# Five more pairs of merge gates by seven products ahead of the attention, and half of the sparse attention's scales on GpSimd

## The chip, the cores and the metric

The kernel runs on one core of a Trainium2 chip. The metric is the device time of one execution in microseconds (us), from the first to the last instruction and what lies around them. Before the change three runs gave 3183.8, 3187.17 and 3191.8 us; the median, 3187.17 us, is the time before. The engines are called PE (TensorE, matrix products), PEld (its weight loads), DVE (VectorE), ACT (ScalarE), POOL (GpSimd) and SP (SyncE, which here issues the transfers).

## The reference, cut to what matters

Two layers follow each other, each on 1024 tokens of width 1024. In a layer, four branches of width 512 (a gated MLP, a sparse attention in three parts, a forgetting attention, an attention on a memory) are projected up and merged under gates that come from the layer's normed input `h` alone:

```
h = rms_norm(x, g_pre)
parts = jnp.split(h @ w_in, IN_SPLITS, axis=-1)
...
ys = jnp.stack([y_a, y_b, y_c, y_m], axis=2)
up = jnp.einsum('bsnw,nwd->bsnd', ys, w_br)
gates = jax.nn.sigmoid(jnp.einsum('bsd,dne->bsne', h, w_gate))
merged = jnp.einsum('bsnd,bsnd->bsd', gates, up)
return x + rms_norm(merged @ w_o, g_post)
```

In the sparse attention the local part looks back over 256 keys, and its probabilities are weighed by a gate of their own:

```
o = g[..., 0:1] * o_cmp + g[..., 1:2] * o_sel + g[..., 2:3] * o_win
```

## The kernel before, in words

All products are in fp32 quality: a number is split in a high and a low part (`hi` by ACT, `lo = x - hi` by DVE or POOL), and three products stand for one (`mm3`, L244, L247, L248). A weight of 128 x 1024 is loaded by `weight` (512 KB), copied by ACT (L220) and subtracted on POOL (L222).

A layer has four stages. **Front** (`front`): norms and the memory's keys. **Gates** (`gates`, L1190 on): the values and projections that need only `h`, and merge gates made ahead of time. **Attention** (`attention`): the forgetting attention (`fox`), then the sparse attention (`nsa`) with the memory attention between. **Merge** (`merge`): the four branches are projected up (L244 to L248 into tiles `s`), multiplied by the gates' tanh and summed, then the output projection.

A merge gate is a 1024 x 128 column block of `w_gate` (branch n, block e, 32 of them) times all 1024 tokens. There are two ways to it. The plain way (`gate_early`, `proj`) takes 2 x 24 products of 128x512, 96 for a pair of neighbours. The other (`gate_pair`, L447) makes a pair by seven products of quarters instead of eight (Strassen's scheme as Winograd orders it): 7 x 12 = 84 products of 128x512, from sums of the tokens' quarters (made once a layer) and of the weights (`weight_sums`: four DVE sums, then seven ACT copies L438 and seven POOL subtractions L439 of 128x512 a pair). Both ways write the tanh to DRAM (`gate_store`), where the merge fetches it (L1281); a gate that no one made ahead is computed in the merge. `FRONT` lists the pairs made in the gates stage: nine of sixteen before. `FILL` lists what is computed beside the sparse attention, in this order: `u` (gated MLP, 96 products), `c`, `m`, `b` (output gates, 48 products each), and `w`, `y` (merge gates of branches 0 and 2, the plain way, 48 each). Before, that is 28 entries and 4 x 96 + 24 x 48 = 1536 products a layer; one gate (branch 2, block 5) is left to the merge.

A scheduler orders each engine's instructions when the program is built, earlier code first where it can. `follow` holds the fill back: each half projection of it (12 products) must stand behind a mark in the attention's score products, so that the fill is spread over the sparse attention's course and runs ahead of its even share by a few marks at most (`SLACK`).

A unit of the sparse attention (`nsa_unit`: one head, 256 queries) makes scores on PE (L565, L566, tiles `s`), masks and reduces them on DVE (L570, tiles `p`), takes exponentials on ACT (L575), multiplies by the reciprocal sum and the gate (`scale`, L640), turns blocks of `p` on PE (L597, tiles `pt`), splits them by ACT and DVE (L306, L308, tiles `pt2`) and multiplies them with the values (L609, tile `o`). There are 32 units a layer, and each scales the selected part and the local part (`win`), two query blocks each.

Of the kernel before, what the change touches and what calls it, by code (L numbers as in the profile page):

```python
# [187 lines left out]
STEP, SLACK = 4, 5.0  # L188


FILL = "u0 y6 y7 c0 y0 u1 w2 w3 m0 c1 b0 u2 w4 y1 m1 w5 c2 b1 u3 w6 w7 m2 y2 b2 c3 y3 m3 y4"

FRONT = [(0, 0)] + [(n, e) for n in (3, 1) for e in range(0, 8, 2)]


def ahead(items, n):
# [8 lines left out]
class Net:  # L207
# [412 lines left out]
        nc.gpsimd.tensor_add(t[r, 0], t[r, 0], t[r, 1])  # L620
        nc.sync.dma_start(dst[r, j * 256:(j + 1) * 256], t[r, 0])

    def scale(self, pcs, l, gate=(None, None)):

        nc = self.nc
        r = self.psm.tile([128, 2], F32, name="r")
        if len(pcs[0]) == len(pcs[1]) == 1:
            nc.vector.reciprocal(r, l[:, :, 0])
        elif len(pcs[0]) == 1:
            nc.vector.tensor_add(l[:, 1, 0:1], l[:, 1, 0:1], l[:, 1, 1:2])  # L630
            nc.vector.reciprocal(r, l[:, :, 0])
        else:
            nc.vector.tensor_add(r, l[:, :, 0], l[:, :, 1])
            nc.vector.reciprocal(r, r)
        for x in range(2):
            for t, b0, n in pcs[x]:
                if gate[x] is None:
                    nc.vector.tensor_scalar_mul(t[:, :n], t[:, :n], r[:, x:x + 1])  # L638
                else:
                    nc.vector.tensor_scalar(t[:, :n], t[:, :n], r[:, x:x + 1], gate[x], op0=OP.mult, op1=OP.mult)  # L640

    def put_values(self, name, h0):

# [309 lines left out]
    def nsa_unit(self, g, h, j, q, kd, kl, v, pc, dst):  # L953
        nc = self.nc
        l = self.psm.tile([128, 2, 2, 2], F32, name="l4")
        nm = self.psm.tile([128, 2, 2, 4], F32, name="nm4")
        sel, win = [], []
        for x in range(2):
            i = 2 * j + x
            def bias(b0, n, i=i):  # L960
                out = []
                m = min(n, i * 128 - b0)
                if m > 0:
                    s = self.selb[:, i - 4, b0 // 64:(b0 + m) // 64] if i >= 4 else self.zero16[:, :m // 64]
                    out.append((0, m, s[:, :, None].to_broadcast([128, m // 64, 64])))
                if b0 + n == (i + 1) * 128:
                    out.append((n - 128, 128, self.tri))
                return out
            sel.append(self.scores(q, kd[0], kl[0], i, 0, (i + 1) * 128, bias, nm[:, 0, x], l[:, 0, x]))
            k0 = max(0, i - 2) * 128  # L970
            wb = lambda b0, n, i=i: [(0, n, self.win[:, 384 - n:384])]
            win.append(self.scores(q, kd[1], kl[1], i, k0, (i + 1) * 128, wb, nm[:, 1, x], l[:, 1, x]))
        hd = (4 * g + h) * 3
        gate = lambda b: [self.sg[:, 2 * j + x, hd + 1 + b:hd + 2 + b] for x in range(2)]
        self.scale(sel, l[:, 0], gate(0))
        o = self.po.tile([128, 2, 256], F32, name="o")
        def blk(pcs, x, b):
            for t, b0, n in pcs[x]:
                if b0 <= b * 128 < b0 + n:
                    return t[:, b * 128 - b0:b * 128 - b0 + 128]  # L980
        it = lambda pcs, s, b, xs: dict(t=[(x, blk(pcs, x, b)) for x in xs], v=v[s][:, b, :])
        items = [dict(t=[(None, pc[:, 2 * j:2 * j + 2, :].rearrange("p i c -> p (i c)"))], v=self.vcm[:, :, g])]
        items += [it(sel, 0, b, (0, 1)) for b in range(2 * j + 1)] + [it(sel, 0, 2 * j + 1, (1,))]
        first = len(items)
        if j:
            items += [it(win, 1, 2 * j - 2, (0,)), it(win, 1, 2 * j - 1, (0, 1)),
                      it(win, 1, 2 * j + 1, (1,)), it(win, 1, 2 * j, (0, 1))]
        else:
            items += [it(win, 1, 1, (1,)), it(win, 1, 0, (0, 1))]
        items[first]["pre"] = lambda: self.scale(win, l[:, 1], gate(1))  # L990
        self.turn_and_sum(o, items)
        self.head_out(o, h % 2, j, dst)

# [205 lines left out]
    def gates(self):  # L1199
        sums = self.token_sums()  # L1200
        self.turn2 = 0
        next(sums)
        self.gmlp_w()
        self.gmlp_v(0)
        next(sums)
        self.gmlp_v(1)
        next(sums)
        self.put_values("cv0", 0)
        next(sums)
        self.put_values("cv1", 4)  # L1210
        next(sums, None)
        self.gmlp_sums()
        self.fox_proj(0)
        w = ahead((x for n, e in FRONT for x in self.weight_sums(f"g{n}{e}", f"g{n}{e + 1}")), 3)
        self.logits()
        for k, (n, e) in enumerate(FRONT):
            self.gate_pair(n, e, w, lambda: self.gmlp_mix(k - 1) if k else self.forget())

    def attention(self):
        self.cmp_proj()  # L1220
# [9 lines left out]
        for name in names:  # L1230
            h = int(name[1])
            if name[0] == "u":
                self.gmlp_u(h)
            elif name[0] in "wy":
                self.gate_early({"w": 0, "y": 2}[name[0]], h)
            else:
                self.gate_out(*{"c": (2, "cz"), "m": (3, "mz"), "b": (1, "bz")}[name[0]], h)
        self.pace = None
# [182 lines left out]
```

## Time and profile before

| what | us |
|---|---|
| median of three runs | 3187.17 |
| the profiled execution | 3185.2 |
| its span, first to last instruction | 3183.4 |
| PE busy in the span | 3071.0 |
| DVE, ACT, POOL busy | 1845.6, 1484.6, 1433.3 |

The busy time of PE is the time in which at least one product was under way. Products overlap, so a product's own duration (0.39 us for 128x512) is longer than its distance to the next one; what a product costs in a dense stretch is read from the starts of neighbours in the timeline. In the views by stretch a column gives an engine's busy time and its instructions; the two layers look alike, and stretches are given for the first: gates 195 to 390, forgetting attention about 449 to 720, sparse attention about 735 to 1310, merge to 1510.

### The profile page before, as it was taken

The numbers are of one execution on the slowest core, as the hardware profiler recorded it, in microseconds if no ns is written. First come the engines' busy times: TensorE is split into PE (matmuls) and PEld (weight loads), VectorE is DVE, ScalarE is ACT, GpSimd is POOL, SyncE is SP. The second block draws the span as 40 slices with busy tenths as digits, with TensorE's granted clock in tenths as the row PEclk, the third lists the DMA queues.
The fourth block names the chain that finished last, engine by engine and source line by source line (L and its number), as shares of the span: only waits on it lengthen the run. The fifth ranks groups of instructions, "written<-read, shape, count | busy, mean of one in ns | idle before, by whom it ended". The sixth has DMA issues, their size and how long they took to land.

```text
span 3183.4 us, 48317 instructions
## 1 busy us (share of the span) xinstructions
PE 3071.0 (96%) x16704; PEld 2633.9 (83%) x16704; DVE 1845.6 (58%) x4329; ACT 1484.6 (47%) x3393; POOL 1433.3 (45%) x1142
## 2 busy tenths in 40 slices
PE   6999999999999999999989999999999999999998
PEld 6978877887888888788989788888888888887888
DVE  6255447768666855336551554477685678554363
ACT  4333335556556555313443433455665556552132
POOL 6744445543232323258557444445432333232673
PEclk9999999999999999999999999999999999999999
DMA  6334485654334322456553344955632342225454
GB/s 206 101 116 133 135 249 172 189 179 131 103 104 147 109 90 93 149 173 197 193 180 105 113 135 146 276 160 175 192 123 83 107 153 99 98 90 184 156 185 140
DMA packets 251685, 466.96 MB, mean 147 GB/s; under 512 B 42512, under 2 KB 100880, under 8 KB 251440
## 3 DMA queue, kind: packets, MB, share of 16 engines
q1 hardware_dynamic: 251440, 463.87, 45.7%
q8 instruction: 132, 2.16, 0.3%
q14 instruction: 113, 0.93, 0.1%
HBM read 326.35 MB, written 137.43 MB: 146 GB/s over the span
## 4 chain that ended last, share of the span: by engine, by line
PE 78%; DVE 5%; POOL 5%; issue 4%; DMA 4%; ACT 3%; SPq 1%; DVEq 0%; POOLq 0%; ACTq 0%
PE pj L244 12%; PE pj L248 12%; PE pj L247 12%; PE s L247 6%; PE s L244 6%; PE s L248 6%; PE s L447 5%; PE o L609 5%; PE pt L597 5%; PE pj L447 4%; PE s L565 3%; PE s L566 3%; POOL wl L222 2%; DVE p L638 1%; POOL acc L1291 1%
## 5 line engine op out<-in xcount | busy, mean ns | idle before, releaser
L222 POOL TENSOR_TENSOR wl<-wr,wh 128x1024 fp32r<-128x1024 f32 (+1 forms) x216 | 515.9, 2392 | 646.5 <-ACT wh L220 562.5
L244 PE MATMUL pj<-hh,wh 128*128 128x512 f32 x1648 | 651.4, 395 | 2.6 <-DVE z L317 1.5
L248 PE MATMUL pj<-hh,wl 128*128 128x512 f32 x1648 | 651.4, 395 | 1.6 <-POOL wl L222 1.6
L247 PE MATMUL pj<-hl,wh 128*128 128x512 f32 x1648 | 649.7, 394 | 0.0
L575 ACT ACTIVATE p<-p,nm 128x384 f32<-128x384 f32 (+3 forms) x512 | 306.8, 601 | 204.3 <-DVE nm L570 201.3
L308 DVE TENSOR_TENSOR pt<-pt,pt 128x512 fp32r<-128x512 f32 (+1 forms) x464 | 292.4, 635 | 147.7 <-ACT pt L306 146.1
L248 PEld LDWEIGHTS pj<-hh,wl 128*128 128x128 f32 x1648 | 310.2, 188 | 61.6 <-POOL wl L222 2.5
L244 PEld LDWEIGHTS pj<-hh,wh 128*128 128x128 f32 x1648 | 310.8, 189 | 60.8 <-DVE z L317 2.4
L247 PEld LDWEIGHTS pj<-hl,wh 128*128 128x128 f32 x1648 | 310.4, 188 | 57.7
L306 ACT ACTIVATE pt<-pt 128x512 fp32r<-128x512 f32 (+1 forms) x464 | 251.9, 554 | 222.8 <-PE pt L597 162.2
L220 ACT ACTIVATE wh<-wr 128x1024 fp32r<-128x1024 f32 x216 | 228.4, 1057 | 248.0 <-PE pj L247 84.8
L609 PE MATMUL o<-pt,v 128*128 128x512 f32 (+1 forms) x864 | 245.2, 370 | 7.6 <-DVE pt L308 7.3
L618 POOL TENSOR_TENSOR yt<-yt 128x256 f32<-128x256 f32 x128 | 100.6, 786 | 292.7 <-ACT yt L617 232.8
L597 PE MATMUL pt<-ident,p 128*128 128x128 f32 x1488 | 230.9, 272 | 0.3
L597 PEld LDWEIGHTS pt<-ident,p 128*128 128x128 f32 x1488 | 184.9, 140 | 42.5 <-DVE pt L308 0.7
L244 PE MATMUL s<-yh,wh 128*128 128x512 f32 x512 | 199.9, 393 | 7.1 <-ACT yh L306 5.3
L247 PE MATMUL s<-yl,wh 128*128 128x512 f32 x512 | 201.0, 393 | 1.5 <-DVE yl L310 1.4
L248 PE MATMUL s<-yh,wl 128*128 128x512 f32 x512 | 200.3, 391 | 0.0
L565 PE MATMUL s<-kd,q 128*128 128x512 f32 (+2 forms) x512 | 187.5, 369 | 13.1 <-DVE nm L570 13.1
L566 PE MATMUL s<-kl,q 128*128 128x512 f32 (+2 forms) x512 | 175.7, 345 | 0.0
L609 PEld LDWEIGHTS o<-pt,v 128*128 128x128 f32 x864 | 147.6, 188 | 32.0 <-DVE pt L308 12.3
L640 DVE TENSOR_SCALAR p<-p,r,sg 128x384 f32<-128x384 f32 (+2 forms) x320 | 167.0, 577 | 1.7
(370 smaller groups left out, 7143.1 us busy)
## 6 DMA issues: line engine op xcount, KB each, us to landing
wr<-wt SPq DMA_DIRECT2D x234, 512.0 KB
th<-thd SPq DMA_DIRECT2D x124, 256.0 KB
thd<-gu SPq DMA_DIRECT2D x72, 256.0 KB
q<-rq SPq DMA_DIRECT2D x32, 512.0 KB
yf<-y SPq DMA_DIRECT2D x64, 256.0 KB
thd<-th SPq DMA_DIRECT2D x52, 256.0 KB
vd<-vs SPq DMA_DIRECT2D x48, 256.0 KB
v<-vd SPq DMA_DIRECT2D x24, 512.0 KB
```

Source lines behind the costliest of these rows:

```text
L222: nc.gpsimd.tensor_sub(lo[:, :n], raw[:, :n], hi.bitcast(F32)[:, :n])
L244: ins = nc.tensor.matmul(out, ah, bh, start=k == 0, stop=False)
L247: nc.tensor.matmul(out, ah, bl, start=False, stop=False)
L248: nc.tensor.matmul(out, al, bh, start=False, stop=k == n - 1)
L306: self.last_act = nc.scalar.activation(hi, src, AF.Copy, scale=scale)
L308: (nc.gpsimd if pool else nc.vector).tensor_sub(lo, src, hi.bitcast(F32))
L447: nc.tensor.matmul(out, w[a][:, k], t[b][:, k], start=start and k == x == 0, stop=k == 3 and x == 2, skip_group_check=True)
L565: self.mark(nc.tensor.matmul(ps[:, :w], q[:, tq], kd[:, b0:b0 + w], start=True, stop=False), 1 + n / 128)
L566: nc.tensor.matmul(ps[:, :w], q[:, tq], kl[:, b0:b0 + w], start=False, stop=True)
L575: nc.scalar.activation(p[:, :n], p[:, :n], AF.Exp, bias=init, scale=-1.0, accum_out=l[:, x:x + 1])
L597: nc.tensor.transpose(pt[:, off + x * 128:off + x * 128 + 128], src, self.ident)
L609: nc.tensor.matmul(o[:, :, t0:t0 + m], it["v"], w[:, :, off:off + m], start=first, stop=last)
```

## The change

`FRONT` gets five pairs more: fourteen of sixteen are made by seven products ahead of the attention. `FILL` loses the six `w` and three of the seven `y` entries; four `y` remain (blocks 6, 7, 4, 5 of branch 2), so all 32 gates are now made before the merge. The fill is 19 entries, 4 x 96 + 15 x 48 = 1104 products a layer. In `nsa_unit` the local part's two scales run on POOL (`pool=True`); its selected part stays on DVE.

```diff
-FILL = "u0 y6 y7 c0 y0 u1 w2 w3 m0 c1 b0 u2 w4 y1 m1 w5 c2 b1 u3 w6 w7 m2 y2 b2 c3 y3 m3 y4"
+FILL = "u0 y6 c0 u1 m0 c1 b0 u2 y7 m1 c2 b1 u3 m2 y4 b2 c3 m3 y5"
-FRONT = [(0, 0)] + [(n, e) for n in (3, 1) for e in range(0, 8, 2)]
+FRONT = [(n, e) for n in (0, 3, 1) for e in range(0, 8, 2)] + [(2, 0), (2, 2)]
...
-    def scale(self, pcs, l, gate=(None, None)):
+    def scale(self, pcs, l, gate=(None, None), pool=False):
         nc = self.nc
+        by = nc.gpsimd if pool else nc.vector
...
-                    nc.vector.tensor_scalar(t[:, :n], t[:, :n], r[:, x:x + 1], gate[x], op0=OP.mult, op1=OP.mult)
+                    by.tensor_scalar(t[:, :n], t[:, :n], r[:, x:x + 1], gate[x], op0=OP.mult, op1=OP.mult)
...
-        items[first]["pre"] = lambda: self.scale(win, l[:, 1], gate(1))
+        items[first]["pre"] = lambda: self.scale(win, l[:, 1], gate(1), pool=True)
...
-            self.gate_pair(n, e, w, lambda: self.gmlp_mix(k - 1) if k else self.forget())
+            self.gate_pair(n, e, w, lambda: self.gmlp_mix(k - 1) if 0 < k <= 8 else None if k else self.forget())
...
-            elif name[0] in "wy":
-                self.gate_early({"w": 0, "y": 2}[name[0]], h)
+            elif name[0] == "y":
+                self.gate_early(2, h)
```

The built order of PE in the middle of the sparse attention, before. Rows with `pj` are fill; `s` are scores, `pt` turned blocks, and `pt_8638` is the split copy of a turned bank.

```order
L565 MATMUL s<-kd,q 128x384
L566 MATMUL s<-kl,q 128x384
L244 MATMUL pj<-hh_501,wh 128x512
L247 MATMUL pj<-hl_503,wh 128x512
L248 MATMUL pj<-hh_501,wl 128x512
L597 MATMUL pt<-ident,p 128x128 x4
L565 MATMUL s<-kd,q 128x384
L566 MATMUL s<-kl,q 128x384
L244 MATMUL pj<-hh_501,wh 128x512
L247 MATMUL pj<-hl_503,wh 128x512
L605 MATMUL o<-pt_8638,vcm 128x2x128 x2
L609 MATMUL o<-pt_8638,v 128x512
```

The same engine in the middle of the sparse attention of the changed kernel, in one of the places where the fill has run out.

```order
L597 MATMUL pt<-ident,p 128x128 x8
L605 MATMUL o<-pt_9175,vcm 128x2x128 x2
L609 MATMUL o<-pt_9175,v 128x512
L565 MATMUL s<-kd,q 128x256
L566 MATMUL s<-kl,q 128x256
L565 MATMUL s<-kd,q 128x384
L566 MATMUL s<-kl,q 128x384
L609 MATMUL o<-pt_9186,v 128x512 x2
L597 MATMUL pt<-ident,p 128x128 x4
L609 MATMUL o<-pt_9196,v 128x512 x2
L597 MATMUL pt<-ident,p 128x128 x4
L565 MATMUL s<-kd,q 128x512
```

Where two or three fill products stood between a turned bank and the product that reads its split copy, only the unit's own scores and turns stand now.

The built order of POOL between the two groups of heads, before:

```order
L618 TENSOR_TENSOR yt<-yt 128x256
L620 TENSOR_TENSOR yt<-yt 64x256
L222 TENSOR_TENSOR wl<-wr,wh 128x1024
L618 TENSOR_TENSOR yt<-yt 128x256
L620 TENSOR_TENSOR yt<-yt 64x256
L618 TENSOR_TENSOR yt<-yt 128x256
L620 TENSOR_TENSOR yt<-yt 64x256
```

And there in the changed kernel:

```order
L618 TENSOR_TENSOR yt<-yt 128x256
L620 TENSOR_TENSOR yt<-yt 64x256
L641 TENSOR_SCALAR p<-p,r,sg 128x384 x2
L222 TENSOR_TENSOR wl<-wr,wh 128x1024
L618 TENSOR_TENSOR yt<-yt 128x256
L620 TENSOR_TENSOR yt<-yt 64x256
L918 TENSOR_TENSOR pc<-pc,cl 128x512
```

A unit's two local scales stand as a pair in POOL's queue, between the head outputs (`yt`) and the fill's weights (`wl`).

## Rows read from the trace of the kernel before

**Rows 1.** The page's first part: busy time, share and instructions of each engine.

```profile
PE 3071.0 (96%) x16704; PEld 2633.9 (83%) x16704; DVE 1845.6 (58%) x4329; ACT 1484.6 (47%) x3393; POOL 1433.3 (45%) x1142
```

**Rows 2.** Busy time by stretch; columns as its first line names them.

```profile
core 0: us, PE busy (x) PEld busy (x) DVE busy (x) ACT busy (x) POOL busy (x), PEclk, DMA share, GB/s
250.00:400.00 150.00, 150.00 (x705) 125.61 (x704) 70.65 (x130) 54.18 (x90) 71.02 (x57) 1.00 0.44 144
760.00:1300.00 540.00, 537.88 (x2817) 455.68 (x2818) 356.11 (x1011) 297.89 (x769) 161.02 (x126) 1.00 0.33 108
```

**Rows 3.** Timeline of PE in the gates: start us, us, engine, line, operation.

```profile
252.66 0.39 PE L447 MATMUL pj<-t3h,wh 128*128 128x512 f32 x1
252.89 0.39 PE L447 MATMUL pj<-t3l,wh 128*128 128x512 f32 x1
```

**Rows 4.** Groups by line, whole span: busy us, mean ns | idle before.

```profile
L439 POOL TENSOR_TENSOR wl<-ws,wh 128x512 fp32r<-128x512 f32 x72 | 98.1, 1375 | 103.6 <-ACT wh L438 67.3 <-PE s L447 33.0 <-PE pj L447 3.3
```

**Rows 5.** Groups by line and shape of DVE, 760 to 1300 us.

```profile
L308 DVE TENSOR_TENSOR pt<-pt,pt 128x512 fp32r<-128x512 f32 x94 | 64.3, 686 | 38.6 <-ACT pt L306 38.0
L640 DVE TENSOR_SCALAR p<-p,r,sg 128x384 f32<-128x384 f32 x64 | 38.1, 626 | 0.3
...
L570 DVE CUSTOM_DVE_ANT_1 p<-s,selb 128x512 f32<-128x512 f32 x32 | 22.0, 687 | 17.9 <-PE pt L597 12.7 <-PE s L566 4.4 <-PE pt L1152 0.5
...
L640 DVE TENSOR_SCALAR p<-p,r,sg 128x256 f32<-128x256 f32 x24 | 12.7, 530 | 0.0
...
L640 DVE TENSOR_SCALAR p<-p,r,sg 128x128 f32<-128x128 f32 x24 | 9.9, 412 | 0.3
...
L628 DVE RECIPROCAL r<-l 128x2 f32<-128x2 f32 x48 | 7.1, 157 | 2.5 <-ACT p L575 2.5
```

**Rows 6.** The scale's line, whole span: duration ns min/median/max.

```profile
L640 DVE TENSOR_SCALAR p<-p,r,sg x320: 331/478/2771, 764.2 to 2868.3; 128x384 f32<-128x384 f32 x64, 128x512 f32<-128x512 f32 x64, 128x128 f32<-128x128 f32 x32
```

**Rows 7.** Timeline of DVE at 775 us.

```profile
774.86 0.54 DVE L640 TENSOR_SCALAR p<-p,r,sg 128x512 f32<-128x512 f32 x1
...
775.65 3.38 DVE L640 TENSOR_SCALAR p<-p,r,sg 128x384 f32<-128x384 f32 x2
```

**Rows 8.** Timeline of POOL at 775 us.

```profile
775.25 2.75 POOL L222 TENSOR_TENSOR wl<-wr,wh 128x1024 fp32r<-128x1024 f32 x1 [12.53 <-PE pt L597]
```

**Rows 9.** Groups by line and shape of POOL, whole span.

```profile
L618 POOL TENSOR_TENSOR yt<-yt 128x256 f32<-128x256 f32 x128 | 100.6, 786 | 292.7 <-ACT yt L617 232.8 <-issue 58.3 <-POOL yt L620 1.5
...
L818 POOL MEMSET vcm<- 128x512 f32 x2 | 1.1, 526 | 0.0
```

**Rows 10.** Groups by line and shape of ACT, 760 to 1300 us.

```profile
L306 ACT ACTIVATE pt<-pt 128x512 fp32r<-128x512 f32 x92 | 54.1, 597 | 64.5 <-PE pt L597 47.1 <-PE o L609 6.4 <-PE pt L1152 6.1
L575 ACT ACTIVATE p<-p,nm 128x384 f32<-128x384 f32 x64 | 39.2, 613 | 19.2 <-DVE nm L570 18.9
L575 ACT ACTIVATE p<-p,nm 128x512 f32<-128x512 f32 x48 | 34.4, 718 | 19.5 <-DVE nm L570 19.5
...
L575 ACT ACTIVATION_READ_ACCUMULATOR p<-p,nm 128x1 f32 x160 | 30.3, 189 | 0.0
```

**Rows 11.** Timeline of PE at the end of the sparse attention.

```profile
1300.19 0.62 PE L609 MATMUL o<-pt,v 128*128 128x512 f32 x2
...
1304.83 0.74 PE L609 MATMUL o<-pt,v 128*128 128x512 f32 x2 [0.48 <-DVE pt L308]
...
1309.64 0.62 PE L609 MATMUL o<-pt,v 128*128 128x256 f32 x2 [0.56 <-DVE pt L308]
```

**Rows 12.** Timeline of PE at the start of the sparse attention.

```profile
721.31 0.51 PE L609 MATMUL o<-pt,v 128*128 128x256 f32 x2
...
727.31 0.45 PE L244 MATMUL pj<-hh,wh 128*128 128x512 f32 x1
```

**Rows 13.** Busy time by stretch where PE stands still and just behind.

```profile
1310.00:1313.00 3.00, 0.36 (x3) 0.10 (x1) 0.12 (x1) 1.79 (x4) 1.45 (x2) 1.00 0.00 0
1313.00:1316.50 3.50, 3.41 (x8) 2.38 (x9) 3.50 (x6) 3.49 (x7) 0.00 (x0) 0.52 0.48 150
```

## Prediction, made before the run

> **What bounds the kernel now.** First the page's busy shares [rows 1]: PE is busy in 96% of the span, no other engine in more than 58%. A share is an average over stages, so next the busy times by stretch [rows 2]. In the gates PE is busy in all of 150 us, with DVE, POOL and ACT at half or less. In the sparse attention it is busy in 537.9 of 540 us, DVE in 356.1, ACT in 297.9, POOL in 161.0. So both stages that the change touches are bound by PE today: work taken from PE there shortens the kernel, work moved between DVE and POOL does not by itself. Third, the timeline for the price of a product: a product of 128x512 is under way for 0.39 us, but its neighbour starts 0.227 us (252.89 less 252.66, with the rounding of the rows) behind it [rows 3]. A product that goes is worth 0.227, not 0.39.
>
> **The products.** Five pairs a layer change from 96 products to 84: 60 a layer and 120 in all, 120 x 0.227 = 27.2 us less. By place, for one layer: the gates gain 5 x 84 x 0.227 = 95.3 us, the fill loses 432 x 0.227 = 98.1 us, the merge loses the one gate left to it, 48 x 0.227 = 10.9 us. In the gates one pair lasts 84 x 0.227 = 19.1 us on PE; beside it POOL has seven subtractions of 1.375 us, 9.6 us [rows 4], and DVE and ACT have spare time at the shares of [rows 2], where nine such pairs already run back to back. I cost the new pairs' sums, copies and subtractions at nothing; without that cover the 9.6 us would still be half of what PE needs. Transfers: each pair loads the same two weights as before, earlier, through the same SP queue, and its four tanh tiles are stored either way; only the gate that the merge used to make adds two stores and two loads of 256 KB a layer. DMA is busy 0.44 of its time in the gates [rows 2], so I cost that at nothing too.
>
> **The scales.** 64 a layer go from DVE to POOL: 48 of 128x384, 8 of 128x256, 8 of 128x128, at 626, 530 and 412 ns [rows 5], 37.6 us less on DVE in each sparse attention. POOL's price for this operation is in no row. Below: writing 128x512 without reading took 526 ns; above: two inputs and 128x256 took 786 ns and 128x512 took 1375 [rows 4, 9], so 1.08 for 128x384. I take 0.9 us, near the subtractions, between 0.4 and 1.1. POOL's load is then 161 + 58 us less nine weights, still under half of its time. The scale stands between exponential and turn: by the built order, at the spacing of the rows, the turn of a local tile comes 28 us of PE work behind the score product (median of 128; 7.7 us at the least). The chain has a reduction, an exponential, a reciprocal and two scales, some 3.5 us. So the move costs PE nothing unless POOL's queue is late by several us; behind a scale in it stand head outputs and fill weights, which PE needs much later. At 0.4 or 1.1 us the sum is the same.
>
> The Trainium skill ("GPSIMD Engine Reference", section 4.1, Engine selection) says that GpSimd is about twice as slow as DVE with two inputs and roughly at line rate with one. By it the scale would take nearer the lower end, and the sum would be unchanged; no run so far shows it.
>
> **What the fill hid.** This is the term that decides. The fill falls from 1536 to 1104 products, and `follow` spreads it evenly over the score products; so where a unit has more to wait for than its share of fill covers, PE has nothing else. The built order shows it: in the first layer's sparse attention there are now nine places where 4 to 8 us of attention stand without a fill product, 54.0 us of issue together, by the spacings of the rows; before there was one of 4.9 us, and the last units at the end, which both kernels have. In such a place a bank is turned, copied by ACT in 0.60 us and subtracted by DVE in 0.69 [rows 5, 10], and the product that reads it stands 0.8 to 1.5 us of PE work behind the turn.
>
> Its price has three rows of evidence. (a) The end of the sparse attention today: from 1300.19 to the last `o` product at 1309.64, which ends its issue by 1309.98, 6.6 us of issue took 9.8 us, 0.48 lost for each us [rows 11]. There DVE has nothing else to do. (b) The one place in mid-stage: 4.9 us of issue took 6.0 (721.31 to 727.31), 0.22 [rows 12]. (c) The place of 8.2 us whose order the section on the change shows, walked by hand: behind the copy of its third bank ACT has two exponentials (0.61 + 0.19 + 0.72 + 0.19), then DVE two reciprocals (0.31), two scales (0.48 + 0.54), a reduction (0.69) and only then the fourth bank's subtraction (0.69), 4.4 us; PE has 2.0 us of its own work until the product that needs it. It is late by 2.4 us, and behind it DVE keeps up: 0.28 or 0.29 for each us. I take 0.28, from the very kind of place in question: 54.0 x 0.28 = 15.1 us a layer, 30.2 in two, less 2 x 1.1 that the one place of today loses: 28 us more waiting. Bounds: nothing, if banks and scores happen to be ready, and 0.48, which gives 51.8 - 2.2 = 50 us.
>
> **The sum** against the profiled execution, 3185.2 us: -27.2 + 28 = +1, so 3186. The median of the three runs lies 2.0 above that execution, so 3188 us: no change that can be told. For this kernel about 0.3% (9.6 us) is what a measurement can tell from none, 3177.6 to 3196.7.
>
> **Rivals.**
>
> *The fill was not needed.* The waits of PE in the sparse attention are 2 us of 540 today, DVE has a third of its time free [rows 2] and loses 38 us more of work. If the places without fill lose only what today's mid-stage place (b) loses or less (0 to 0.22, 0 to 22 us), the time is 3160 to 3182; with half of (b), 3185.2 - 27.2 + 10 + 2 = 3170. For it: the subtractions and scores mostly come well ahead of their readers. Against it: (a) and (c). Chance 0.30.
>
> *PE stands bare and slows down besides.* One mechanism, at the nine places of each layer: they cost (a)'s 0.48, 50 us, and the longer stops bring the lower clock. Today PE stands from 1310 to 1313 us, and the granted clock is 0.52 in the 3.5 us behind [rows 13], the lower of its two levels (1.2 of 2.4 GHz) for most of it, some 1.7 us lost. Eighteen places with a third of them so punished add 10 us. The time: 3185.2 - 27.2 + 50 + 2 = 3210, with the clock 3220. It decides from 0.36 lost for each us on, where the waits pass the 37 us that make the sum slower by over 0.3%. Chance 0.27.
>
> *POOL's scales hold up DVE.* At 775.25 a subtraction of 2.75 us starts on POOL, and DVE's two scales that start at 775.65 take 3.38 us together [rows 7, 8], where the median of one is 0.478 and the longest 2.771 [rows 6]: they stand until POOL has done. If each new scale on POOL holds DVE for its 0.9 us, DVE gets 58 us of standing a layer for the 38 us of work it gave. Only what falls in the 54 of some 450 us without fill reaches PE: 7 us a layer. 3188 + 14 = 3202. Against it: the DVE reductions and bank subtractions read one input from PSUM, and their rows hardly spread. Chance 0.05.
>
> The Trainium skill ("SBUF — State Buffer", section Who interferes with whom) has this as an exclusive lock: a DVE instruction in a two-port mode, `tensor_scalar` among them, and a GpSimd instruction block each other fully. The trace agrees for the 2.75 us subtraction at 775.25 and the scale behind it; by that rule the third rival's 14 us would be the most it costs here.
>
> **How the numbers follow.** The wash, 3178 to 3197, has 0.38 and the first rival 0.30, the second 0.27, the third 0.05. Faster by over 0.3%: the first rival and a little of the wash, 0.33. Within 0.3%: the rest of the wash, 0.36. Slower: the second and third and a little of it, 0.31. The likeliest case's time is 3188; its own range is 3178 to 3197. To hold the time 8 times in 10 the range reaches into the first two rivals, 3163 to 3214.
>
> **What would show it.** Products of L447 go from 1512 to 2352, those of L244, L247 and L248 fall by 960, and the gates last 95 us longer a layer with PE busy throughout; if PE waits for `wl` or `wh` of L438 and L439 there, the cover fails. The sparse attention should take about 450 us plus some 15 of waits, where the waits of `o` L609 for `pt` L308 and of `s` L565 for `nm` L570 grow from 2 us to over 10. If these stay at 2 us, the first rival holds; at 25 with more stretches of lowered clock, the second. POOL's L641 should last about 0.9 us for 128x384, and no transposition should wait for it; if `pt` L597 waits for POOL, the step on the scales is wrong. What would make the whole wrong is a merge or a forgetting attention that changes by more than the 11 us of its gate.

## The result, and the profile after

The changed kernel takes 3224.8 us (median of 4 runs, 3223.2 to 3233.7), beside 3187.2 us for the kernel before: 1.0116 of it, 95% interval 1.0097 to 1.0135. It is slower by some 37 us, where 3188 was forecast, and outside the range of 3163 to 3214. Four runs of 4344 us and more (two of the kernel before, one each of those with 8 and 7 pairs further down) were slow as a whole and are in none of the medians.

The first part of the page, changed kernel; it answers to [rows 1]:

```profile
PE 3070.7 (95%) x16584; PEld 2622.1 (81%) x16584; DVE 1863.6 (58%) x4291; ACT 1510.5 (47%) x3453; POOL 1570.2 (49%) x1320
```

PE makes 120 products fewer and is busy for the same 3071 us, in a span of 3221.6 in place of 3183.4 us: it stands 150.9 us in place of 112.4, and products that stand alone or run at a lower clock last longer (the mean of L609 went from 370 to 380 ns). The busy times by stretch tell where it stands. First the same stretch of the gates as in [rows 2], then the sparse attention of the first layer from its first to its last score product, changed kernel:

```profile
core 0: us, PE busy (x) PEld busy (x) DVE busy (x) ACT busy (x) POOL busy (x), PEclk, DMA share, GB/s
250.00:400.00 150.00, 150.00 (x705) 125.62 (x704) 73.45 (x135) 54.63 (x95) 72.11 (x60) 1.00 0.41 135
...
818.10:1307.60 489.50, 464.37 (x2461) 388.62 (x2459) 356.08 (x1002) 294.76 (x819) 195.31 (x189) 0.99 0.33 104
```

And the second of these in the kernel before:

```profile
725.40:1282.60 557.20, 553.03 (x2910) 468.69 (x2909) 378.59 (x1064) 315.83 (x848) 173.83 (x138) 1.00 0.34 110
```

The gates are as dense as before. In the sparse attention PE stands 25.1 us, where it stood 4.2; DVE's share rises from 0.68 to 0.73, though it has 22.5 us less to do, because the stage got shorter by 67.7 us.

What PE waits for most in that stretch, changed kernel (who waits <- for whom: us in all, times, the longest):

```profile
PE o L609 <- DVE pt L308: 10.8, 7, 3.7
PE s L565 <- DVE nm L570: 4.3, 5, 1.5
PE o L605 <- DVE pt L308: 4.3, 5, 1.6
PE s L901 <- DVE pc L903: 2.1, 1, 2.1
```

These four are 21.5 of the 25.1 us, and all of them are waits for DVE: the split of a turned bank (L308), the reduction that frees a bank of scores (L570), the masking of the compressed scores (L903). None is a wait for a scale on POOL.

To set stage against stage, the distance of each product to the next one is split into its issue (0.227 us for 128x512, less for the smaller ones, from the dense stretches) and the rest, at full and at lowered clock apart. The waits of this table are thus more than PE's standing: what a product takes beyond its issue counts too. This is worked out from all rows of PE in both traces; the first layer's merge reaches to the second layer's gates. Change from before to after, in us, first layer / second layer:

| stage | issue | waits at full clock | waits at lowered clock |
|---|---|---|---|
| gates | +95.3 / +95.3 | -0.1 / -0.3 | 0 / 0 |
| forgetting attention | -2.7 / -2.7 | +0.9 / +1.6 | +1.1 / 0 |
| sparse attention | -100.7 / -100.3 | +28.0 / +28.4 | +5.0 / +6.5 |
| merge | -5.5 / -5.9 | -4.2 / -1.4 | +1.7 / -0.4 |

So the products went as counted, and of the 201 us of issue that the two sparse attentions were spared a third came back as waits, 67.9 us, while the gates took their 190.6 in full.

The longest single stop, at 901.7 us, shows how it comes about. Timeline of all engines but the weight loads, changed kernel (start us, us, engine, line, operation, [idle before <- releaser]):

```profile
895.19 1.48 POOL L641 TENSOR_SCALAR p<-p,r,sg 128x384 f32<-128x384 f32 x2 [2.87 <-DVE r L629]
895.25 4.60 DVE L641 TENSOR_SCALAR p<-p,r,sg 128x512 f32<-128x512 f32 x4
...
896.51 1.09 ACT L306 ACTIVATE pt<-pt 128x512 fp32r<-128x512 f32 x2 [0.26 <-PE pt L597]
...
896.64 2.47 POOL L222 TENSOR_TENSOR wl<-wr,wh 128x1024 fp32r<-128x1024 f32 x1
...
897.72 0.28 PE L566 MATMUL s<-kl,q 128*128 128x256 f32 x1
...
899.77 0.67 DVE L317 SCALAR_TENSOR_TENSOR z<-z,pj 128x512 f32<-128x512 f32 x1
900.37 0.68 DVE L1134 TENSOR_REDUCE mm<-s 128x2 f32<-128x512 f32 x1
...
900.97 1.27 DVE L308 TENSOR_TENSOR pt<-pt,pt 128x512 fp32r<-128x512 f32 x2
...
901.70 1.22 PE L609 MATMUL o<-pt,v 128*128 128x512 f32 x2 [3.70 <-DVE pt L308]
```

The bank that PE needs is turned at 896.5 and copied by ACT. DVE has four scales in its queue that last 4.60 us, then a step of an output gate (L317) and a reduction of the memory attention (L1134), and only then the bank's subtraction. PE has its own work until 898.0 and no fill behind it. The four scales last longer than the 2.5 us that four of 623 ns took on the mean in the kernel before; POOL's two scales and its subtraction of 2.47 us run at the same time, so POOL has a part in this stop.

The same in the 4 us ahead of four of the stops: DVE is busy in 0.90 to all of them, where its mean over the stage is 0.73. Busy time by stretch, changed kernel:

```profile
897.70:901.70 4.00, 0.30 (x4) 0.10 (x2) 4.00 (x6) 0.00 (x0) 2.59 (x2) 0.83 0.78 253
847.20:851.20 4.00, 0.97 (x7) 0.63 (x5) 4.00 (x6) 1.64 (x4) 3.55 (x3) 1.00 0.24 62
869.80:873.80 4.00, 2.66 (x18) 2.13 (x17) 3.61 (x9) 1.47 (x3) 2.71 (x3) 1.00 0.16 59
825.60:829.60 4.00, 1.88 (x12) 1.30 (x10) 4.00 (x10) 1.40 (x3) 1.45 (x3) 1.00 0.40 147
```

The granted clock of 0.83 in the first of them says that the lower of the two levels (1.2 and 2.4 GHz) set in while PE stood.

The scales, by line and shape in the sparse attention of the changed kernel: POOL's, then DVE's, which answer to [rows 5].

```profile
L641 POOL TENSOR_SCALAR p<-p,r,sg 128x384 f32<-128x384 f32 x46 | 36.6, 804 | 80.2 <-DVE r L629 46.4 <-DVE r L635 19.0 <-PE pt L597 7.5
...
L641 DVE TENSOR_SCALAR p<-p,r,sg 128x512 f32<-128x512 f32 x45 | 37.0, 834 | 0.5
```

In the kernel before DVE's 128x512 took 623 ns in the same stretch:

```profile
L640 DVE TENSOR_SCALAR p<-p,r,sg 128x512 f32<-128x512 f32 x45 | 27.4, 623 | 0.3
```

### The profile page after: what moved, and what is told of

Same layout as the page of the kernel before. It is cut to its first block, busy times and chain, and to the rows that moved or that the text cites. A ratio compares the mean times of both kernels' runs of the same rounds, so it can differ in the third digit from the quotient of the medians.

```text
span 3221.6 us, 48552 instructions
## 1 busy us (share of the span) xinstructions
PE 3070.7 (95%) x16584; PEld 2622.1 (81%) x16584; DVE 1863.6 (58%) x4291; ACT 1510.5 (47%) x3453; POOL 1570.2 (49%) x1320
## 4 chain that ended last, share of the span: by engine, by line
PE 74%; DVE 10%; issue 4%; DMA 4%; POOL 4%; ACT 3%; SPq 1%; DVEq 0%; POOLq 0%; ACTq 0%
PE pj L244 9%; PE s L447 9%; PE pj L247 9%; PE pj L248 9%; PE pj L447 6%; PE s L244 6%; PE s L247 6%; PE s L248 6%; PE o L609 4%; PE pt L597 4%; PE s L565 2%; PE s L566 2%; DVE p L641 1%; DVE pt L308 1%; POOL wl L222 1%
## 5 line engine op out<-in xcount | busy, mean ns | idle before, releaser
L222 POOL TENSOR_TENSOR wl<-wr,wh 128x1024 fp32r<-128x1024 f32 (+1 forms) x196 | 468.9, 2397 | 332.8 <-ACT wh L220 313.6
L244 PE MATMUL pj<-hh,wh 128*128 128x512 f32 x1328 | 526.9, 397 | 0.9 <-DVE z L317 0.9
L248 PE MATMUL pj<-hh,wl 128*128 128x512 f32 x1328 | 524.3, 395 | 0.0
L247 PE MATMUL pj<-hl,wh 128*128 128x512 f32 x1328 | 523.8, 394 | 0.0
L308 DVE TENSOR_TENSOR pt<-pt,pt 128x512 fp32r<-128x512 f32 (+1 forms) x464 | 290.9, 634 | 108.7 <-ACT pt L306 107.0
L220 ACT ACTIVATE wh<-wr 128x1024 fp32r<-128x1024 f32 x196 | 206.9, 1056 | 202.3 <-PE s L247 82.5
L248 PEld LDWEIGHTS pj<-hh,wl 128*128 128x128 f32 x1328 | 250.5, 189 | 50.0
L244 PEld LDWEIGHTS pj<-hh,wh 128*128 128x128 f32 x1328 | 251.4, 189 | 47.0 <-DVE z L317 1.3
L247 PEld LDWEIGHTS pj<-hl,wh 128*128 128x128 f32 x1328 | 251.0, 189 | 46.0
L609 PE MATMUL o<-pt,v 128*128 128x512 f32 (+1 forms) x864 | 253.9, 380 | 29.2 <-DVE pt L308 29.0
L597 PE MATMUL pt<-ident,p 128*128 128x128 f32 x1488 | 235.1, 275 | 0.3 <-DVE pt L308 0.3
L597 PEld LDWEIGHTS pt<-ident,p 128*128 128x128 f32 x1488 | 187.6, 141 | 43.8 <-issue 1.5
L439 POOL TENSOR_TENSOR wl<-ws,wh 128x512 fp32r<-128x512 f32 x112 | 149.7, 1348 | 134.7 <-ACT wh L438 98.2
L565 PE MATMUL s<-kd,q 128*128 128x512 f32 (+2 forms) x512 | 192.3, 378 | 20.8 <-DVE nm L570 19.1
L609 PEld LDWEIGHTS o<-pt,v 128*128 128x128 f32 x864 | 145.7, 191 | 54.7 <-DVE pt L308 30.4
L641 POOL TENSOR_SCALAR p<-p,r,sg 128x384 f32<-128x384 f32 (+2 forms) x128 | 95.3, 753 | 192.9 <-DVE r L629 117.2
```

Of the source, the lines that this page charges most:

```text
L220: nc.scalar.activation(hi, raw, AF.Copy)
L222: nc.gpsimd.tensor_sub(lo[:, :n], raw[:, :n], hi.bitcast(F32)[:, :n])
L244: ins = nc.tensor.matmul(out, ah, bh, start=k == 0, stop=False)
L247: nc.tensor.matmul(out, ah, bl, start=False, stop=False)
L248: nc.tensor.matmul(out, al, bh, start=False, stop=k == n - 1)
L308: (nc.gpsimd if pool else nc.vector).tensor_sub(lo, src, hi.bitcast(F32))
```

## The experiments

The theories: **A**, DVE's local backlog, which the fill covered, makes the waits. **B**, POOL's scales hold up DVE. **C**, the even spacing of the fill and not its amount. **E** (later), PE's order is too tight for the chain's latency, whatever DVE has to do. Each time is a median with its ratio to the kernel before on the same chip. DVE's load and the waits at full clock (above those of the kernel before) are of the sparse attention; the load is that of the first layer, the waits are of first / second, and a dash stands where they were not worked out.

| run | pairs | time | ratio, 95% interval | DVE us | waits us |
|---|---|---|---|---|---|
| before | 9 | 3187 | 1 | 378.6 | 0 |
| after | 14 | 3224.8 | 1.0116 (1.0097 to 1.0135) | 356.1 | 28.0 / 28.4 |
| scales back on DVE | 14 | 3233.3 | 1.0147 (1.0132 to 1.0162) | 376.9 | 33.7 / 31.4 |
| scales on POOL alone | 9 | 3191.9 | 1.0016 (1.0006 to 1.0026) | 352.5 | 1.6 / 1.1 |
| all scales on POOL | 14 | 3208.4 | 1.0069 (1.0049 to 1.0090) | 316.6 | 21.6 / 20.4 |
| SLACK 60 | 14 | 3221.7 | 1.0115 (1.0095 to 1.0136) | 351.5 | 26.8 / 27.9 |
| 10 pairs | 10 | 3196.0 | 1.0027 (1.0015 to 1.0038) | 375.2 | 6.5 / 5.4 |
| 11 pairs | 11 | 3204.3 | 1.0053 (1.0037 to 1.0069) | 371.1 | 12.4 / 12.8 |
| 12 pairs | 12 | 3217.0 | 1.0090 (1.0072 to 1.0107) | 371.1 | 20.4 / 17.4 |
| all scales on POOL | 11 | 3198.4 | 1.0034 (1.0022 to 1.0045) | 310.3 | 10.1 / 10.4 |
| no scales | 14 | 3201.5 | 1.0047 (1.0030 to 1.0064) | 306.8 | 19.5 / 19.1 |
| no scales | 9 | 3185.1 | 0.9989 (0.9976 to 1.0003) | 308.4 | -1.7 / -1.0 |
| no ranking | 14 | 3201.5 | 1.0042 (1.0026 to 1.0058) | 333.1 | 19.1 / 21.1 |
| neither | 14 | 3190.5 | 1.0013 (1.0003 to 1.0022) | 288.3 | 14.6 / 11.6 |
| scales made twice | 9 | 3200.6 | 1.0042 (1.0027 to 1.0057) | 421.6 | 8.8 / 9.5 |
| 8 pairs | 8 | 3183.4 | 0.9983 (0.9969 to 0.9997) | 375.5 | -2.8 / -3.1 |
| 7 pairs | 7 | 3171.8 | 0.9957 (0.9943 to 0.9970) | 379.7 | -1.1 / -1.0 |
| 6 pairs | 6 | 3182.6 | 0.9983 (0.9970 to 0.9996) | 365.4 | - |
| 5 pairs | 5 | 3199.5 | 1.0035 (1.0023 to 1.0047) | 375.3 | - |

### Each part alone

The changed kernel with the local scales back on DVE:

```diff
-        items[first]["pre"] = lambda: self.scale(win, l[:, 1], gate(1), pool=True)
+        items[first]["pre"] = lambda: self.scale(win, l[:, 1], gate(1))
```

> The changed kernel (14 pairs ahead) with one part undone: the local branch's 64 scales a layer are on DVE again. Theory A (too little fill is left beside the sparse attention, and what comes last there is DVE's chain): DVE gets back the 22 us a layer that it lost (378.6 us before, 356.6 after, in a sparse attention that is 67 us shorter), all of it in the same bare stretches, so it is no faster than the changed kernel: 3225 to 3250 us. Theory B (POOL's scales hold up DVE, whose own scales of 128x512 went from 617 to 834 ns): the waits of 33 us a layer go back to a few us, 3190 to 3200. PE's waits in a sparse attention: A 28 us or more at full clock, B under 15.

The kernel before with that line the other way round:

> The kernel before (9 pairs ahead) with the other part alone: the local branch's scales on POOL. Theory A: there is fill enough, 2 us of waits a layer cannot shrink by much, 3180 to 3190 us, no change that can be told. Theory B: the same 128 scales hold up DVE here too; part of it is covered by fill, still 3196 to 3210. DVE's scales of 128x512 should go from about 617 to about 830 ns by either.

And the changed kernel with the selected part's scales on POOL too:

```diff
-        self.scale(sel, l[:, 0], gate(0))
+        self.scale(sel, l[:, 0], gate(0), pool=True)
```

> The changed kernel with the selected branch's 96 scales a layer on POOL as well. DVE then has no scale left that POOL can hold up, and loses some 70 us of work a layer (48 at 834 ns, the rest at 0.5 to 0.7 us); POOL gets some 80 us more, 276 of 490 us. Theory A (fill): the bare stretches stay as they are, but DVE's chain in them is shorter by one or two scales of 0.8 us; a third to a half of the 33 us a layer comes back, 3190 to 3210 us. Theory B: nearly all comes back, 3162 to 3180. Third: POOL's queue (1.0 us for a scale of 128x512, head outputs ahead of it) is late, turns wait for POOL, 3225 to 3260.

Measured: 3233.3, 3191.9 and 3208.4 us. The first has 8 us more than the changed kernel, where B asked for some 30 less, so B falls as the cause; with 14 pairs the move to POOL did no harm. With 9 pairs it is 5 us slower. Both differences are within the 0.3% that the prediction takes for no change. DVE's scales of 128x512 went to 697 ns there, not to the 830 that both theories named. With all scales on POOL, 25 us come back of the 46 that the first run lost on the kernel before: A's half, not B's all. The third way in that expectation, POOL's queue late, did not come: no turn in the first layer's sparse attention waits for it.

### Places, not amount

```diff
-STEP, SLACK = 4, 5.0
+STEP, SLACK = 4, 60.0
```

> The changed kernel with the number SLACK that sets how early a fill product may stand ahead of its share raised from 5 to 60: the amount of fill is the same, its places differ. Theory C (not the amount but the even pacing makes the waits): by 15 us or more different from the changed kernel, 3190 to 3210. Theory A (the amount): as many bare stretches in other places, 3215 to 3245. Work is the same in both: same products, same scales.

Measured: 3221.7 us, the same as the changed kernel's. In the built order the first layer's bare stretches of 4 us and more are other ones: five from 11.7 to 16.5 us, 70.9 us of issue that lost 30.0 us, in place of nine up to 8.2 us, 54.0 us that lost 22.5. The loss for each microsecond is the same, 0.42. C falls, as far as this one other spacing can tell: it is the amount.

### Pairs one by one

From the kernel before, with all scales on DVE, one to three pairs of branch 0 go from the fill to the front (three shown):

```diff
-FILL = "u0 y6 y7 c0 y0 u1 w2 w3 m0 c1 b0 u2 w4 y1 m1 w5 c2 b1 u3 w6 w7 m2 y2 b2 c3 y3 m3 y4"
+FILL = "u0 y6 y7 c0 y0 u1 m0 c1 b0 u2 y1 m1 c2 b1 u3 m2 y2 b2 c3 y3 m3 y4"
-FRONT = [(0, 0)] + [(n, e) for n in (3, 1) for e in range(0, 8, 2)]
+FRONT = [(0, 0)] + [(n, e) for n in (3, 1) for e in range(0, 8, 2)] + [(0, 2), (0, 4), (0, 6)]
...
```

> The kernel before with one pair more ahead (10, the pair of gates 2 and 3 of branch 0), all scales on DVE. 24 products less, -5.4 us by count. Theory A1 (a place without fill costs from about 4 us on): in one layer's sparse attention the order has 14.1 us in such places, none before; at 0.42 lost per us, as the changed kernel's nine places showed (22.5 of 54.0), 11.8 us in two layers: +6, 3193. Theory A2 (each pair costs the same from the first on): (3233 - 3187) / 5 = 9.3 us for each: 3196. Theory D (fill is spare at first, the pair is worth its count): 3181.

> The kernel before with two pairs more ahead (11: gates 2, 3 and 6, 7 of branch 0), all scales on DVE; -10.9 us by count. A1: 4.1 us in places of 4 us and more, 3.4 us lost in two layers: -7, 3179. A2: +18.6, 3205. D: 3176. The runs with 10 and 11 pairs tell A1 from D, and the one with 11 tells A1 from A2.

> The kernel before with three pairs more ahead (12: gates 2 to 7 of branch 0), all scales on DVE; -16.3 us by count. A1: 20.8 us in places of 4 us and more, 17.5 lost in two layers: +1, 3188. A2: +28, 3215. D: 3170, if the shortage begins only behind this.

Measured: 3196.0, 3204.3, 3217.0 us; A2 (3196, 3205, 3215) on all three. A1 held for 10 pairs only by chance: with 11 pairs the order has a single bare stretch of 4 us, and the waits are 12.6 us a layer all the same. Divided by the pairs moved, the mean waits of the two layers at full clock are 6.0, 6.3 and 6.3 us a pair, and 6.5 with 14 pairs and the scales on DVE. That is the shape of the thing between 9 and 14 pairs: no threshold, but a price for each microsecond of fill from the first one on. A pair takes 19 to 23 us of issue out of each sparse attention, and some 0.3 of it comes back as waits.

With 11 pairs and all scales on POOL:

> 11 pairs ahead as in the run above, and all 160 scales a layer on POOL, as in the run of the changed kernel with all scales there, which took 25 us from the same 14 pairs with the scales on DVE. If DVE's load is what turns a bare stretch into a wait, the gain scales with the waits that are left: by A1 there is little to gain, 3175 to 3185; by A2 about 11 pairs' waits of some 29 us shrink by half, 3185 to 3195. If POOL's queue itself costs time where there is fill enough (the scales on POOL made the kernel with 9 pairs 5 us slower), up to 3200.

3198.4 us: 6 us less than with the scales on DVE, slower than before all the same. The waits at full clock shrink by a fifth, from 12.6 to 10.2 us a layer, and not by the half that A2 had here.

### DVE's load

Two kernels leave out the scaling (14 pairs and 9), one the ranking of blocks, one both:

```diff
-                else:
-                    by.tensor_scalar(t[:, :n], t[:, :n], r[:, x:x + 1], gate[x], op0=OP.mult, op1=OP.mult)
```

```diff
-        for i in range(4):
-            own = im[:, i, :, None].to_broadcast([128, 16, 16])
...
-            nc.vector.reduce_sum(rank[:, i, :], ge, axis=AX.X)
+        nc.vector.tensor_copy(rank, im)
```

> 14 pairs ahead, all scales on DVE as in the run that took 3233 us, and then the 160 scales a layer left out (the probabilities stay unnormalised): DVE loses some 92 us of work a layer, and nothing goes to POOL in its place. Each pair has so far cost 9.3 us from the tenth on, in waits of PE at products whose bank or score DVE had not come to; DVE was busy 0.87 of the 4 us ahead of these waits and 0.76 on the mean. Theory A (DVE's local backlog is what fill covered): of some 34 us of waits a layer two thirds go, 3180 to 3192 us. Rival E (the order is too tight for the chain's latency whatever DVE's load): less than a third goes, 3212 or more. If it comes out at the 3208 of the run with all scales on POOL, POOL's lock and latency cost nothing; below it, they do.

> The kernel before with its 160 scales a layer left out. A and E: waits were 2 us of 540, nothing to gain: 3180 to 3190. Together with the run above it gives the price of a pair where DVE is light: by A about (3186 - 3185) / 5, near 0 for each; by E it stays near 9.

> The changed kernel with the ranking of the blocks left out (20 operations at the start of each group of heads, 22 us of DVE a layer in two bursts; a copy stands in its place, so other blocks are selected). If only the bursts at the group starts cause the waits: 12 us a layer less, 3200. If the backlog is spread over all units: 4 us a layer or less, 3215 to 3222.

> 14 pairs ahead with the 160 scales a layer and the ranking both left out (unnormalised probabilities, other blocks selected): some 114 us of DVE work a layer less than with the scales on DVE. Theory A (DVE's backlog, bursts above all): no scales gave 32 us and no ranking 23 us where each was alone; if they add up, 3233 - 32 - 23 = 3178, with 3160 where all waits go. Rival E (what is left is the chain's latency, whatever DVE's load): the ranking adds little beside the scales, 3195 or more.

Measured: 3201.5, 3185.1, 3201.5 and 3190.5 us. Without scales, 32 of the 47 us that 14 pairs cost with the scales on DVE come back, and a pair costs (3201.5 - 3185.1) / 5 = 3.3 in place of 9.3 us. That is more than E allowed and less than A asked. It is also 7 us below the run with all scales on POOL, so by the expectation POOL's part costs something there, though 7 us is little to go by. The ranking, 23 us of DVE a layer in two bursts, gives 23 us, which is the number named for bursts alone; but the scales, spread over all units, gave 32 as well, so it is neither alone. With both gone 43 us come back, where the sum of the two was 55 and E's bound 38. A holds for the most part; some 13 us of waits a layer remain. What the stretch waits for then (both left out, 818 to 1300 us):

```profile
PE o L605 <- DVE pt L308: 5.3, 3, 3.7
PE s L899 <- DVE pc L901: 2.0, 1, 2.0
PE o L609 <- DVE pt L308: 1.6, 4, 0.5
PE s L565 <- DVE nm L570: 1.6, 4, 0.8
```

The waits on DVE of L609 and L565 are 3.2 us, where the changed kernel had 15.1; those for the first bank of a unit (L605) are no shorter. The longest of these has another cause than DVE's load (timeline of the same run):

```profile
1074.48 1.09 DVE L900 TENSOR_TENSOR pc<-s,cmask 128x256 f32<-128x256 f32 x3 [3.06 <-DMA cmask<-cmask]
1075.49 0.55 DVE L308 TENSOR_TENSOR pt<-pt,pt 128x384 fp32r<-128x384 f32 x1
...
1076.18 0.77 PE L605 MATMUL o<-pt,vcm 128*128 128x256 f32 x2 [3.65 <-DVE pt L308]
```

DVE itself stands for 3.06 us until the mask of the second group of heads (`cmask`) has come, and the bank's split stands behind that masking in its queue; it is busy in 1.72 of the 4 us ahead of the stop. The second layer has the same at 2656.7, with 1.60 us. The other remaining waits stay open: ahead of some DVE is full, ahead of others not.

The counter-test: the kernel before, its fill whole, with each scale made by two operations.

```diff
...
+                elif twice:
+                    nc.vector.tensor_scalar_mul(t[:, :n], t[:, :n], r[:, x:x + 1])
+                    nc.vector.tensor_scalar_mul(t[:, :n], t[:, :n], gate[x])
...
```

> The kernel before (9 pairs, all of its fill) with each of the 160 scales a layer made by two operations in place of one, on DVE: about 92 us of DVE work a layer more, 470 of 557 us. Theory A: DVE's share (0.84) is above that of the kernel with 14 pairs (0.76), so PE waits though the fill is whole; at the price that the scales had with 14 pairs (32 us for 2 x 92) at least 16 us a layer, 3219 or more. Theory F (fill hides DVE's chain as long as there is enough of it, whatever DVE's load): 3187 to 3195.

3200.6 us: above F's 3195 and well below A's 3219. The two operations are each shorter than the one, so DVE got 43 us more a layer, not 92; A's size has to be halved for that, 15 us in place of 32, and then it agrees. PE's waits in the first layer, with no product moved (group by line: busy us, mean ns | idle before):

```profile
L609 PE MATMUL o<-pt,v 128*128 128x512 f32 (+1 forms) x267 | 74.0, 367 | 2.7 <-DVE pt L308 2.6
L565 PE MATMUL s<-kd,q 128*128 128x384 f32 (+2 forms) x160 | 58.2, 367 | 6.9 <-DVE nm L570 6.6 <-ACT p L1141 0.2
```

In the kernel before these were 0.0 and 2.9 us:

```profile
L609 PE MATMUL o<-pt,v 128*128 128x512 f32 (+1 forms) x269 | 73.9, 364 | 0.0
...
L565 PE MATMUL s<-kd,q 128*128 128x384 f32 (+2 forms) x159 | 57.3, 364 | 2.9 <-DVE nm L570 2.9
```

DVE's load alone makes the same waits, which neither E nor F gives. The chain of one tile is longer here too, but no turn (L597) waits for a scale in this stretch: the waits are at banks and scores that DVE comes to late. The price in the first layer is steady: 8.8 us of waits for 43.0 us of DVE here, 14.2 for 70.1 where the scales go (2.3 us of the 33.7 set against are a wait for a transfer), 19.1 for 88.6 where the ranking goes too: 0.20 to 0.22 us for each. In the second layer it is 0.18 to 0.22. Ranking alone, in its bursts, costs 0.39 (8.9 for 23.0) and 0.30. Where the fill is whole there is little to win back: with 9 pairs, 70 us of DVE less gave 1.7 us.

### Fewer pairs

The other way: pairs leave the front and go back to the fill (7 pairs shown; `x` is a gate of branch 1 made the plain way). The eight mixes of the gated MLP, which stand between the pairs, get fewer places too: two of them share the last pair with 8 pairs, and each of the last two, three and four pairs carries two with 7, 6 and 5.

```diff
-FILL = "u0 y6 y7 c0 y0 u1 w2 w3 m0 c1 b0 u2 w4 y1 m1 w5 c2 b1 u3 w6 w7 m2 y2 b2 c3 y3 m3 y4"
+FILL = "u0 x6 x7 w0 w1 y6 y7 c0 y0 u1 w2 w3 m0 c1 b0 u2 w4 y1 m1 w5 c2 b1 u3 w6 w7 m2 y2 b2 c3 y3 m3 y4"
-FRONT = [(0, 0)] + [(n, e) for n in (3, 1) for e in range(0, 8, 2)]
+FRONT = [(n, e) for n in (3, 1) for e in range(0, 8, 2)][:7]
...
```

> One pair fewer ahead than in the kernel before (8: gates 0 and 1 of branch 0 go back to the fill), all scales on DVE; 24 products more, +5.4 us by count. If there is nothing left to cover at 9 pairs: 3193. If each pair goes on costing 9.3 us, as from 9 to 14: 3178, and the kernel before would have too many pairs ahead.

> Two pairs fewer ahead than in the kernel before (7: gates 0 and 1 of branch 0 and gates 6 and 7 of branch 1 go back to the fill); 24 products more than with 8 pairs, 48 more than before, +10.9 us by count. If nothing is left to cover: 3198. If the run with 8 pairs (0.9983 of before) was no accident and each pair goes on giving 5 us: 3177, and this is the fastest version. If 8 pairs were even with 9: 3188 to 3193.

Measured: 3183.4 and 3171.8 us. The run with 8 pairs lay between its two answers. The one with 7 is faster than both kernels, 0.9957 of the one before (0.9943 to 0.9970, a small gain, but clear of noise), with 48 products more. Its profiled span is 3170.0 us, PE busy 3075.0: 4 us more work than before and 17 us less standing. In the sparse attention PE stood only 4 us a layer in the kernel before, so the gain had to be elsewhere too. PE's busy time by stretch, sparse attention and merge of the first layer (its merge with the second layer's front), then of the second; the kernel before:

```profile
core 0: us, PE busy (x), PEclk, DMA share, GB/s
725.40:1282.60 557.20, 553.03 (x2910) 1.00 0.34 110
1282.60:1774.80 492.20, 467.83 (x2884) 0.98 0.52 169
2302.30:2859.70 557.40, 553.11 (x2911) 1.00 0.34 110
2859.70:3175.10 315.40, 306.30 (x1714) 0.99 0.50 164
```

and with 7 pairs:

```profile
683.00:1244.60 561.60, 560.03 (x2940) 1.00 0.33 109
1244.60:1767.80 523.20, 502.07 (x3048) 0.98 0.50 167
2256.80:2818.80 562.00, 560.29 (x2941) 1.00 0.33 109
2818.80:3161.60 342.80, 338.14 (x1877) 1.00 0.49 163
```

PE stands 1.6 and 1.7 us in the sparse attentions (4.2 and 4.3 before) and 21.1 and 4.7 in the merges (24.4 and 9.1). The fill that no longer fits beside the scores now stands behind the last one, some 160 products a layer. What the last merge waited for in the kernel before:

```profile
PE s L244 <- ACT yh L306: 2.6, 1, 2.6
PE s L247 <- POOL wl L222: 2.3, 1, 2.3
PE o L609 <- DVE pt L308: 1.9, 4, 0.6
```

With 7 pairs the first and the last of these are gone: the fill covers the splits of the last units' banks and of the merge's first input (`yh`). Two more runs were to tell how far that goes (6 pairs: `x4 x5` too; 5: `x2 x3` too):

> Three pairs fewer ahead than in the kernel before (6: gates 4 to 7 of branch 1 and 0, 1 of branch 0 go back to the fill); 24 products more than with 7 pairs, +5.4 us by count. The fill that no longer fits beside the scores stands behind the last one, in the merge. Theory G (fill behind the last score covers waits at the end of the sparse attention and in the merge, which were 15 us in two layers less with 7 pairs): little is left to cover there, the count decides, 3176 to 3181. If each pair goes on giving 5 to 13 us: 3160 to 3168.

> Four pairs fewer ahead than in the kernel before (5: gates 2 to 7 of branch 1 and 0, 1 of branch 0 go back to the fill); +10.9 us by count against 7 pairs. Theory G: 3181 to 3189, back near the kernel before. If each pair goes on giving 5 to 13 us: 3147 to 3163.

Measured: 3182.6 and 3199.5 us. The gain ends at 7, as theory G has it, but both times lie above G's. By the ratios the step from 7 to 6 costs 8 us and the next one 17, where the count says 5.4 for each. The traces show where the rest goes: not to the sparse attention, where PE stands for 1.0 to 1.4 us a layer, but to the gates. The gates of the first layer with 5 pairs, then with 7 (columns as in the first such view), and the longest wait of PE in the first of them:

```profile
195.00:320.60 125.60, 113.07 (x513) 91.91 (x512) 79.97 (x131) 50.88 (x80) 55.34 (x44) 0.95 0.32 106
194.70:349.00 154.30, 147.26 (x681) 120.75 (x680) 96.56 (x149) 64.98 (x104) 74.09 (x58) 0.99 0.33 113
PE s L244 <- ACT xh L306: 4.8, 1, 4.8
```

PE stands 12.5 us there and not 7.0, the granted clock is lower, and the two layers' gates are 59.2 us shorter where two pairs a layer count 76.3. The longest wait is for the input of a mix (`xh`). So the runs with fewer pairs change the gates as well, and whether 7 is the best number with the mixes placed otherwise is not shown.

## Why the prediction was wrong

*Bounds and products: right.* The gates last 288.9 us in place of 193.7, +95.2 where 95.3 was worked out, with PE busy in all of the stretch shown. L447 has its 2352 products. The issue of the whole went down by the 27.2 us of the first term. The merges are shorter by 8 us each, the forgetting attention by 1 or 2: inside the 11 us.

*The scales: right, and small.* POOL's 128x384 took 0.80 us (0.9 taken, 0.4 to 1.1 the range), and PE never waited for them. With no scale left on DVE it took 0.68 us, DVE's own 0.63 [rows 5]: so the rule that one input runs roughly at line rate (the Trainium skill, "GPSIMD Engine Reference", section 4.1, Engine selection) agrees with this case, and the other 0.12 us went with DVE's scales. What the third rival was built on is in the trace (DVE's 128x512 from 623 to 834 ns), and DVE's busy time fell by 22.5 us and not by the 37.6 of the scales that it gave away. It is not the cause of the loss: the same 14 pairs without the move are no faster.

*What the fill hid: this step failed.* The term was 54.0 us of bare stretch at 0.28 us lost for each, 30.2 us in two layers, 28 after what is lost today. It measured 67.9, and the other stages changed by little beyond the count. Three things in it were wrong, in this order of weight. First, it counted only nine places of 4 us and more and set the rest at nothing. In the first layer the 37 places of 2 to 4 us (87.5 us) lost 11.9 us, where such places lose 0.6 in the kernel before; and the run with 11 pairs lost 12.4 us with one place of 4 us in the order. Second, the price: the nine places lost 22.5 us, 0.42 for each, between the 0.28 taken and the 0.48 that was the other end. The hand-walked place lost 2.8 us where 2.4 was worked out, so the walk was right, but its place was not the rule: elsewhere DVE had the work of other units and of the fill in its queue besides, as at 901.7. Third, the lowered clock, 11.5 of the 67.9 us, left to a rival; it is contained in the losses just given.

What lies under the first two, as the counter-test and the stretches ahead of the stops suggest, is a reading of a mean: the prediction takes DVE, at 356.1 of 540 us, for an engine with a third of its time free, and its walk of one place finds that DVE keeps up. It is so on the mean and isn't so ahead of the waits. A stretch of the kernel before that the prediction does not use tells it: the 4 us ahead of its longest stop, a wait of 2.9 us for L570 at 760.6, with the fill whole.

```profile
756.60:760.60 4.00, 1.08 (x7) 0.60 (x5) 3.93 (x9) 1.40 (x4) 2.01 (x2) 0.94 0.16 58
```

PE is busy in 1.08 of these 4 us and DVE in 3.93: it is in the ranking of the first group, with a step of the gated MLP between.

*The rivals.* The second, PE stands bare and slows down besides, 3210 to 3220, is the nearest, and its number is in part luck. Its nine places lost 0.42 with the lowered clock in it, where it took 0.48 and 10 us of clock on top; the waits outside of these places, which it had at nothing as well, made up for that. More lowered clock was seen (13.7 us of the first layer's sparse attention, where it was 3.4), but its other sign, 25 us of waits at L609 and L565, was not: they are 15.1, over the 10 that were the sign of the likeliest case. The first rival, fill not needed, is refuted by the run with 10 pairs already, which took 3196 us where spare fill would have given 3181.

## What to carry to other kernels

Work that fills gaps has a price at which it is worth keeping: here, between 9 and 14 pairs, each microsecond of fill taken from beside the attention came back as a third of one in waits, from the first on and without a threshold. So a cheaper form of the same work, which must run elsewhere, has to save more than that share: seven products for eight save an eighth. Judge the engine beside the bound one by its busy share in the few microseconds ahead of a wait and not by its mean, and try the number of moved pieces in both directions before believing that it is the best.

## What the runs showed of the hardware that was not expected

On DVE a multiplication by two numbers a row was longer than one by a single number, and two of the second cost less than twice the first: 128x384 took 627 ns with two scalars in the kernel before, 575 and 505 ns for the two operations in the counter-test; 128x512 took 623 against 490 and 568. POOL works beside them in both runs, and its part in these means was not held apart. A microsecond of DVE work was worth some 0.2 us of PE's waits, put into this stage with its fill whole (DVE at 0.74 of the time) or taken from it with the fill short (from 0.75 to 0.61); taken from it with the fill whole it was worth almost nothing.
